# An attention and long-convolution backbone: value products issued two steps at a time, the exponentials' two half sums added on TensorE, reciprocals on a reshaped tile, the maxima's remainders in pairs, weight scalings on ScalarE

## The chip, the cores and the metric

One core of a Trainium2 chip runs the whole program. The metric is the device time of one execution in microseconds (us), lower is better; the time before is a median of three runs. Engines are named as in the profile: PE (TensorE, with PEld for its weight loads), DVE (VectorE), ACT (ScalarE), POOL (GpSimd), SP (SyncE, which issues the transfers).

## The reference, cut to what matters

Two layers over 1024 latent tokens of width 1024, with 256 context tokens before them as further keys. The first layer is attention, the second a gated long convolution; the change touches the attention alone. Its two kinds of heads have the same core:

```python
def one_block(qi):
    s = jnp.einsum("bqhgd,bkhd->bhgqk", _f32(qi), kf) * scale
    p = jax.nn.softmax(s, axis=-1)
    return jnp.einsum("bhgqk,bkhe->bqhge", p, vf)
...
o_a = block_attention(q_a..., k_a, v_a, GQA_HEAD_DIM ** -0.5)           # 8 heads, 2 key/value heads, width 64
o_m = block_attention(q_m..., k_m, v_m, (MLA_NOPE_DIM + MLA_ROPE_DIM) ** -0.5)   # 8 heads, width 96, values 64
o = jnp.concatenate([o_a..., o_m...], axis=-1)
return (o * jax.nn.silu(gate)) @ w_out
```

There are 1280 keys for each query. All is float32, and the norm weights are drawn large (factors of 8 on `attn_q_norm`, `attn_k_norm` and `mla_q_norm`), so scores are large and a row's maximum has to be subtracted before the exponential.

## The kernel before, in words

Queries stand in columns: a block of scores is [128 keys, 512 queries]. `groups` lists 32 groups, (kind, head, half of the queries): groups 0 to 15 are kind 0 (grouped-query heads), groups 16 to 31 kind 1 (latent heads). A group has five **steps**, each with two key tiles of 128.

One step of `attention()` (L1230 to L1288) does for each of its two key tiles j the score products into one of two [128, 1024] PSUM tiles `pw` (L1253; two passes of fp32r matmuls for kind 0, three for kind 1, so that products of split high and low parts add up to float32), then one exponential on ACT over both tiles (L1261, `PT`), a running sum of the exponentials (`add`, L1169: POOL adds the [128, 1024] tiles of steps 1 to 3, and of step 4 DVE adds one half and POOL the other), and the value products of the step before (`pv`, L1158, in full float32: four matmuls of 64 columns by 256 queries, two side by side in the array). `later` holds the steps whose value products are still to come.

Three further things run inside the steps:

- The **maxima of the next group**, `max_piece` (L980): 12 matmuls per group, for each of four query tiles three widths of keys, 512, 512 and 256, each into a PSUM bank from `pq()` and reduced on DVE (L989). Three of them go with each of steps 0 to 3. `max_all` (L991) reduces the [128, 12] to [128, 4], `max_rows` (L1003) turns that on PE (L1009, a float32 transpose) and DVE writes the negated rows into the next group's queries (L1014), where an extra row of the key operand adds them to the scores.
- The **end of the group before**: `add_last` (L1181) adds the two halves of the sum on DVE into `acs`; `gated` (L1206) multiplies the value products by the gate out of PSUM; `sums` (L1198) adds over keys with four matmuls by ones, one per query tile, side by side in strips of 32 (L1202), and DVE takes the reciprocal of [128, 128] of which four rows are used (L1204); `spread` (L1215) sends those rows to memory and back to 64 partitions; `scale_out` (L1224) multiplies on POOL, two groups later.
- A second generator, `mla_prep` (L1331), makes the latent heads' queries (`nope`, `pe`), keys (`key_stack`, L1308) and values (`Vm`, L1460 to L1479). Each begins with a scaling of weights by a norm vector and a split into a high and a low part. A third, `out_weights`, prepares the output projection's weights.

`Streams` (L70) runs these generators against a clock of estimated costs when the program is written, so the order on each engine is fixed in advance; an engine takes its instructions in that order and waits where one is not ready. A PSUM bank from `pq()` (three in rotation during attention: the fourth holds the value products of two groups, `pv2`) can be written again once its reader is done. Tiles with `bufs=1` (`acc`, `acs`, `R`, `rb`) are written again once the last reader is done.

## Time and profile before

| | |
|---|---|
| median of three runs | 1850.01 us (1847.22 to 1852.31) |
| the profiled execution's own time | 1850.4 us |
| its span in the profile | 1848.5 us |
| attention, groups 0 to 31 | from 490 to 1037 us of the span |
| PE, DVE, ACT, POOL busy over the span | 94%, 61%, 41%, 47% |
| chain of work that ended last | PE 54%, DVE 10%, DMA 5%, POOL 2%, ACT 2% |

"Busy" counts the records' durations. A matmul record lasts longer than the step from one matmul to the next (0.39 us against 0.23 us for 512 columns), because matmuls are pipelined. So the start times of neighbouring PE rows are what tells a matmul's cost, and an idle PE in a table has been waiting a little longer than the table says.

### The profile page before, as it was taken

Reading aid. Unit: us, or ns where it says so; the run is one execution under the profiler, and the core shown is the slowest. Engines: PE = TensorE matmul, PEld = TensorE weight load, DVE = VectorE, ACT = ScalarE, POOL = GpSimd, SP = SyncE. Lnnn points to the kernel's source line nnn. Section 1 sums busy time; section 2 is a strip of 40 time slices with the busy share of each in tenths; the row PEclk is TensorE's granted clock in tenths of the full one; section 3 lists DMA queues with packets and bytes.
Section 4 is the critical chain, followed back from the end, with each engine's and each line's share of the span. In section 5 each row is a group of like instructions: output and inputs, shape, how many; then the busy total and the mean of one; then the engine's idle time right before and its main releaser. Section 6 shows DMA issues by size and latency. Waiting matters only on the chain.

```text
span 1848.5 us, 25379 instructions
## 1 busy us (share of the span) xinstructions
PE 1744.1 (94%) x9360; PEld 1332.5 (72%) x9360; DVE 1136.7 (61%) x1646; ACT 749.9 (41%) x1250; POOL 866.2 (47%) x606
## 2 busy tenths in 40 slices
PE   7899999999999998899999999999999999889898
PEld 2677788977765665565656688888878888778676
DVE  5467657446777877777777423555676666555743
ACT  4878711253544544343443333243333343333332
POOL 2457622443378778566666453234243334334300
PEclk9999999999999999899999999999999999999999
DMA  7776688122120011001000215567778787787623
GB/s 248 231 225 217 201 260 271 56 80 80 36 58 24 13 44 29 27 21 34 19 22 29 77 69 149 166 172 219 219 205 235 227 244 204 204 239 217 202 93 112
DMA packets 243427, 253.18 MB, mean 137 GB/s; under 512 B 28191, under 2 KB 193087, under 8 KB 242887
## 3 DMA queue, kind: packets, MB, share of 16 engines
q1 hardware_dynamic: 241128, 249.47, 45.2%
q10 hardware_dynamic: 2176, 2.10, 0.4%
q8 instruction: 74, 1.21, 0.3%
q14 instruction: 49, 0.40, 0.1%
HBM read 169.65 MB, written 61.94 MB: 125 GB/s over the span
## 4 chain that ended last, share of the span: by engine, by line
PE 54%; DVE 10%; DMA 5%; POOL 2%; ACT 2%; issue 2%; SPq 1%; POOLq 0%; DVEq 0%; ACTq 0%
PE pw L1253 8%; PE pw L103 8%; PE pw L101 8%; PE pw L102 8%; PE pv L1166 6%; PE pq L988 3%; PE pq L101 2%; PE pq L102 2%; PE pq L103 2%; PE pq L1818 2%; DMA K<-Kd 2%; PE pq L1835 2%; DVE mx L989 2%; DMA bd<-cbT 1%; DMA ad<-caT 1%
## 5 line engine op out<-in xcount | busy, mean ns | idle before, releaser
L1261 ACT ACTIVATE PT<-pw 128x1024 f32<-128x1024 f32 x160 | 163.6, 1023 | 218.2 <-PE pw L1253 210.1
L989 DVE TENSOR_REDUCE mx<-pq 128x1 f32<-128x512 f32 (+1 forms) x384 | 215.5, 594 | 42.3 <-PE pq L988 38.7
L101 PE MATMUL pw<-h1h,wh 128*128 128x512 f32 x512 | 209.6, 409 | 0.0
L103 PE MATMUL pw<-h1h,wl 128*128 128x512 f32 x512 | 202.5, 396 | 3.6 <-POOL wl L1676 3.6
L102 PE MATMUL pw<-h1l,wh 128*128 128x512 f32 x512 | 200.8, 392 | 0.0
L1811 POOL TENSOR_TENSOR K<-K,skp 128x512 f32<-128x512 f32 x64 | 85.4, 1336 | 217.7 <-DMA K<-Kd 210.9
L1175 POOL TENSOR_TENSOR acc<-acc,PT 128x1024 f32<-128x1024 f32 x62 | 147.7, 2383 | 35.9 <-ACT PT L1261 33.7
L103 PEld LDWEIGHTS pw<-h1h,wl 128*128 128x128 f32 x512 | 96.5, 188 | 25.7 <-POOL wl L1676 4.3
L1821 DVE SCALAR_TENSOR_TENSOR cB<-pq,K 64x512 f32<-64x512 f32 x64 | 44.3, 693 | 110.6 <-PE pq L1818 36.6
L547 POOL TENSOR_TENSOR kacc<-kacc,kabs 128x512 f32<-128x512 f32 x56 | 72.2, 1289 | 83.8 <-ACT kabs L545 81.9
L102 PEld LDWEIGHTS pw<-h1l,wh 128*128 128x128 f32 x512 | 97.3, 190 | 17.9
L101 PEld LDWEIGHTS pw<-h1h,wh 128*128 128x128 f32 x512 | 97.3, 190 | 17.5
L1173 POOL TENSOR_TENSOR acc<-PT,PT 128x1024 f32<-128x1024 f32 x31 | 73.7, 2377 | 74.3 <-DVE acs L1184 63.7
L1676 POOL TENSOR_TENSOR wl<-wr,wh 128x1024 fp32r<-128x1024 f32 x32 | 78.6, 2455 | 54.5 <-ACT wh L1675 36.2
L1791 ACT COPY caT<-pq 128x512 f32<-128x512 f32 x64 | 37.6, 587 | 142.0 <-PE pq L103 101.9
L1166 PE MATMUL pv<-PT,Va 128*64 128x256 f32 x640 | 86.7, 392 | 2.3 <-DVE gT L1212 2.3
L1166 PE MATMUL pv<-PT,Vm 128*64 128x256 f32 x640 | 85.9, 391 | 0.0
L1852 DVE TENSOR_TENSOR cil<-spare,cih 128x512 fp32r<-128x512 f32 x64 | 57.1, 930 | 42.2 <-ACT cih L1851 42.2
L573 PE MATMUL pq<-au,FBk 128*128 128x256 f32 x256 | 68.3, 391 | 11.8 <-DVE kc L584 11.6
L1818 PE MATMUL pq<-cau,FB 128*128 128x128 f32 x512 | 69.7, 280 | 8.9 <-DVE cA L1824 7.9
L1835 PEld LDWEIGHTS pq<-cA,GB 128*128 128x128 f32 x512 | 67.6, 193 | 12.3 <-issue 7.1
L1837 ACT COPY cbT<-pq 128x512 f32<-128x512 f32 x64 | 37.3, 587 | 95.9 <-PE pq L1835 53.0
(444 smaller groups left out, 4727.1 us busy)
## 6 DMA issues: line engine op xcount, KB each, us to landing
K<-Kd SPq DMA_DIRECT2D x128, 256.0 KB
au<-aT SPq DMA_DIRECT2D x128, 128.0 KB
space<-in_ada_w_dram SPq DMA_DIRECT2D x32, 512.0 KB
wr<-in_hy_w_in_dram SPq DMA_DIRECT2D x32, 512.0 KB
ad<-caT SPq DMA_DIRECT2D x64, 256.0 KB
cau<-ad SPq DMA_DIRECT2D x32, 512.0 KB
bd<-cbT SPq DMA_DIRECT2D x32, 512.0 KB
spare<-bd SPq DMA_DIRECT2D x64, 256.0 KB
```

The costliest lines, as they stand in the source:

```text
L101: nc.tensor.matmul(ps, lh, rh, start=start, stop=False)
L102: nc.tensor.matmul(ps, lh, rl, start=False, stop=False)
L103: nc.tensor.matmul(ps, ll, rh, start=False, stop=stop)
L989: nc.vector.reduce_max(mxs[gi][:, p:p + 1], ps[:, :w], axis=AX.X)
L1166: nc.tensor.matmul(ps[64 * e:64 * e + 64, 0:256], vals[:, 2 * s + j], PT[:, j, 256 * e:256 * e + 256], start=s == 0 and j == 0, stop=s == ...
L1175: eng.tensor_tensor(accs[gi], accs[gi], PT, ALU.add)
L1253: nc.tensor.matmul(ps[:, 512 * j:512 * j + 512], l[:, kt * P:(kt + 1) * P], r, start=i == 0, stop=i == len(passes) - 1)
L1261: nc.scalar.activation(PT, ps.rearrange("p (a q) -> p a q", q=512), AF.Exp, scale=SC_A if kind == 0 else SC_M)
L1676: nc.gpsimd.tensor_tensor(wl, f(r), f(wh), ALU.subtract)
L1811: nc.gpsimd.tensor_tensor(K[:, 0], K[:, 0], B["skp"].unsqueeze(1).to_broadcast([P, 4, P]), ALU.add)
L1818: nc.tensor.matmul(ps[:, i * P:(i + 1) * P], FB[:, 4 * uc + i, :], au[:, 4 * (uc % 2) + i, :], start=True, stop=True)
L1835: nc.tensor.matmul(ps[:, i * P:(i + 1) * P], GB[:, 4 * uc + i, :], A1[:, i, :], start=True, stop=True)
```

## The change

- **Value products** are issued in bursts: where `(group + step)` is odd, those of the two oldest waiting steps; otherwise none (group 16: in steps 1 and 4).
- **Sums**: `add_last` and `acs` are gone. `sums` takes both halves of `acc` (now two buffers) as eight matmuls that accumulate, and stands in step 3 of an even group and step 2 of an odd one.
- **Reciprocals**: ACT copies the [128, 128] out of PSUM, a transfer brings the four used rows to [32, 16], DVE takes the reciprocal of that two steps or more later (`inverse`, in step 0), and `spread` follows from there. `scale_out` moves from step 0 to step 3. Groups 30 and 31 keep the old way.
- **Maxima**: the 256-wide remainders of two query tiles share one bank and one reduction (12 reductions become 10); pieces go as two or three per step, with one behind the burst; `max_all` moves from step 4 to the end of step 3, and the transpose in `max_rows` stands between the two key tiles' scores of step 4. In step 0 the first pass of both key tiles, which doesn't read the new rows, is issued ahead of the second.
- **Scalings**: the scalings by norm vectors go from DVE to ACT, the low parts of `ukl` and `uvl` from DVE to POOL, the high part in `nope` and half of the copies of `Vm` from DVE to ACT.

```diff
-    def max_piece(gi, p):
+    def max_piece(gi, i, j):
...
+        if j < 2:
+            nc.tensor.matmul(ps, tile_(i), K[:, 512 * j:512 * j + 512], start=True, stop=True)
+            nc.vector.reduce_max(m[:, i, j:j + 1], ps, axis=AX.X)
+        else:
+            for e in range(2):
+                nc.tensor.matmul(ps[:, 256 * e:256 * e + 256], tile_(i + e), K[:, 1024:1280], start=True, stop=True)
+            nc.vector.tensor_reduce(m[:, i:i + 2, 2], ps.rearrange("p (e k) -> p e k", e=2), AX.X, ALU.max)
...
-                accs[gi] = ap_.tile([P, 2, 512], F32, tag="acc", bufs=1, name=nm("acc"))
+                accs[gi] = ap_.tile([P, 2, 512], F32, tag="acc", bufs=2, name=nm("acc"))
...
-        def add_last(gi):
-            a = accs[gi]
-            accs[gi] = ap_.tile([P, 512], F32, tag="acs", bufs=1, name=nm("acs"))
-            nc.vector.tensor_tensor(accs[gi], a[:, 0], a[:, 1], ALU.add)
...
-            for i in range(4):
-                nc.tensor.matmul(pr[32 * i:32 * i + 32, 0:P], ones[:, 0:32], a[:, i * P:(i + 1) * P], start=True, stop=True)
-            Rs[gi] = ap_.tile([P, P], F32, tag="R", bufs=1, name=nm("R"))
-            nc.vector.reciprocal(Rs[gi], pr[:, 0:P])
+            for e in range(2):
+                for i in range(4):
+                    nc.tensor.matmul(pr[32 * i:32 * i + 32, 0:P], ones[:, 0:32], a[:, e, i * P:(i + 1) * P], start=e == 0, stop=e == 1)
+            R = ap_.tile([P, P], F32, tag="R", bufs=1, name=nm("R"))
...
+                nc.scalar.copy(R, pr[:, 0:P])
+                Rs[gi] = ap_.tile([32, 16], F32, tag="rc", bufs=2, name=nm("rc"))
+                nc.sync.dma_start(Rs[gi], R[0:P:32, :].rearrange("a (b q) -> a b q", q=16))
+
+        def inverse(gi):
+
+            rc = Rs.pop(gi)
+            nc.vector.reciprocal(rc, rc)
+            spread(gi, rc)
...
-                olds = [later.pop(0) for _ in range(len(later) - keep)]
+                burst = s in (1, 4) if gi == 16 else (gi + s) % 2
+                olds = [later.pop(0) for _ in range(len(later) - 1)] if burst else []
...
+                if s == 0:
+                    for j in range(2):
+                        scores(j, todo[:1])
+                    todo = todo[1:]
+                scores(0, todo)
...
                 if s == 0 and gi > 1:
+                    inverse(gi - 2)
+                if s == 3 and gi > 1:
                     scale_out(gi - 2)
...
-                if s == 1 and gi > 0:
-                    add_last(gi - 1)
+                if s == 1 + gi % 2 and gi > 0:
                     gated(gi - 1)
-                if s == 2 and gi > 0:
+                if s == 3 - gi % 2 and gi > 0:
                     sums(gi - 1)
...
+    def scaled_parts(wh, wl, r, k):
+
+        nc.scalar.activation(r, r, AF.Identity, scale=k)
+        nc.scalar.copy(wh, r)
+        nc.gpsimd.tensor_tensor(wl, r, f(wh), ALU.subtract)
...
-                    nc.vector.tensor_copy(A[0:64, c], raw)
+                    nc.scalar.copy(A[0:64, c], ps[b_])
...
-        nc.vector.tensor_scalar(r, r, kw, 0.0, ALU.mult, ALU.add)
+        nc.scalar.activation(r, r, AF.Identity, scale=kw)
...
-        nc.vector.tensor_tensor(uvl, r, f(uvh), ALU.subtract)
+        nc.gpsimd.tensor_tensor(uvl, r, f(uvh), ALU.subtract)
...
-            evac(Vm[:, kt, :], ps)
+            nc.scalar.copy(Vm[:, kt, :], ps)
```

Over the whole program the matmuls by ones go from 128 to 256 and no other product is added or removed. DVE loses 151 of its 1648 instructions, ACT gains 76 and POOL 9, and SP issues 30 more transfers.

**PE, group 7, from the sums of group 6 to the first scores of group 8, before.** `pw` are scores, L988 the maxima's pieces, L1202 the sums, L1166 value products (x4 is one step), L1009 the transpose of the maxima.

```order
L1202 MATMUL pq_5705<-acs_5679,ones 32x128 x4
L1253 MATMUL pw_5717<-Qa_4199,K_4188 128x512
L1253 MATMUL pw_5717<-Q_4194,K_4190 128x512
...
L988 MATMUL pq_5731<-K_4189,Qa_4200 128x256
L1166 MATMUL pv_4631<-PT_5667,Va 64x256 x4
L1253 MATMUL pw_5738<-Qa_4199,K_4188 128x512
...
L1009 MATMUL pq_5747<-ident,m_1097_5741 4x128
L1166 MATMUL pv_4631<-PT_5691,Va 64x256 x4
L1253 MATMUL pw_5755<-Qa_4200,K_4189 128x512
```

**The same place in the change.** L1277 are scores, L989 and L993 the pieces, L1212 the sums, L1180 value products, L1023 the transpose.

```order
L989 MATMUL pq_5694<-K_4189,Qa_4200 128x512
L1212 MATMUL pq_5699<-acc_5568,ones 32x128 x8
L1277 MATMUL pw_5713<-Qa_4199,K_4188 128x512
...
L989 MATMUL pq_5723<-K_4189,Qa_4200 128x512
L1277 MATMUL pw_5730<-Qa_4199,K_4188 128x512
L1277 MATMUL pw_5730<-Q_4194,K_4190 128x512
L1023 MATMUL pq_5733<-ident,m_1076_5727 4x128
L1277 MATMUL pw_5730<-Qa_4199,K_4188 128x512
L1277 MATMUL pw_5730<-Q_4194,K_4190 128x512
L1180 MATMUL pv_4627<-PT_5665,Va 64x256 x4
L1180 MATMUL pv_4627<-PT_5678,Va 64x256 x4
L1277 MATMUL pw_5749<-Qa_4200,K_4189 128x512 x2
```

The transpose stood directly ahead of value products, two matmuls of scores and one step of value products behind the last piece; now it stands between scores, two matmuls behind the last piece. In odd groups a piece also stands between the value products and the sums; in even groups the sums follow the value products directly. Counted over the attention, the unbroken runs of float32 matmuls among the fp32r ones go from 158 (125 of value products with or without sums, 31 with a transpose ahead, 2 of sums alone) to 127 (79 of value products, 17 of sums alone, 31 of a transpose alone).

**POOL, groups 14 and 15, before** (`acc` the running sums of exponentials `PT`; `gT<-gT,rb` is `scale_out`):

```order
L1173 TENSOR_TENSOR acc_6699<-PT_6641,PT_6670 128x1024
L1175 TENSOR_TENSOR acc_6699<-acc_6699,PT_6694 128x1024
L1175 TENSOR_TENSOR acc_6699<-acc_6699,PT_6728 128x1024
L1179 TENSOR_TENSOR acc_6699<-acc_6699,PT_6748 128x512
L1228 TENSOR_TENSOR gT<-gT,rb_6717 64x512
L1173 TENSOR_TENSOR acc_6819<-PT_6767,PT_6790 128x1024
```

**The same in the change:**

```order
L1187 TENSOR_TENSOR acc_6699<-PT_6641,PT_6661 128x1024
L1189 TENSOR_TENSOR acc_6699<-acc_6699,PT_6694 128x1024
L1250 TENSOR_TENSOR gT<-gT,rb_6651 64x512
L1189 TENSOR_TENSOR acc_6699<-acc_6699,PT_6710 128x1024
L1193 TENSOR_TENSOR acc_6699<-acc_6699,PT_6752 128x512
L1187 TENSOR_TENSOR acc_6815<-PT_6764,PT_6796 128x1024
```

`scale_out` now stands ahead of the group's last full addition, whose result DVE's half addition (L1192 in the change) reads in step 0 of the next group.

## Rows read from the trace of the kernel before

**Rows 1.** The page's first part: busy time of each engine, share of the span, instructions.

```profile
PE 1744.1 (94%) x9360; PEld 1332.5 (72%) x9360; DVE 1136.7 (61%) x1646; ACT 749.9 (41%) x1250; POOL 866.2 (47%) x606
```

**Rows 2.** Busy time by stretch: the stretch around group 16, and the sum over 490 to 1037 us, which is the attention (length, busy us of each engine, and in the first row the granted clock, DMA share and GB/s).

```profile
738.00:780.00 42.00, 33.33 (x158) 22.52 (x159) 29.56 (x41) 16.80 (x23) 19.61 (x11) 0.88 0.09 33
...
sum 547.00, PE 518.15 PEld 327.29 DVE 415.68 ACT 231.67 POOL 387.05; mean PE 172.72 PEld 109.10 DVE 138.56 ACT 77.22 POOL 129.02
```

**Rows 3.** PE in order of time in group 7, where no other work is mixed in: start us, us, engine, line, what, count. Two records stand for each float32 matmul, so x8 is four of them.

```profile
601.96 0.51 PE L988 MATMUL pq<-K,Qa 128*128 128x512 f32 x2
602.40 1.08 PE L1166 MATMUL pv<-PT,Va 128*64 128x256 f32 x8
603.41 0.43 PE L1202 MATMUL pq<-acs,ones 128*32 128x128 f32 x8
603.77 0.50 PE L1253 MATMUL pw<-Qa,K 128*128 128x512 f32 x1
604.11 0.39 PE L1253 MATMUL pw<-Q,K 128*128 128x512 f32 x1
604.34 0.39 PE L988 MATMUL pq<-K,Qa 128*128 128x512 f32 x1
...
607.51 0.27 PE L1009 MATMUL pq<-ident,m 128*4 128x128 f32 x1
607.72 1.08 PE L1166 MATMUL pv<-PT,Va 128*64 128x256 f32 x8
...
609.29 0.39 PE L988 MATMUL pq<-K,Qa 128*128 128x512 f32 x1
```

**Rows 4.** PE in order of time in group 16, where the value products of three steps follow each other.

```profile
766.80 2.81 PE L1166 MATMUL pv<-PT,Vm 128*64 128x256 f32 x24
769.54 0.45 PE L101 MATMUL pq<-ckh,ukh 128*64 128x512 f32 x1
```

**Rows 5.** What PE waited for between 490 and 1037 us: who <- what, us in total, times, longest.

```profile
PE pq L1202 <- DVE mx L989: 11.7, 8, 3.2
PE pq L988 <- DVE mx L989: 5.1, 9, 1.0
PE pq L102 <- DVE uvl L1472: 3.1, 1, 3.1
...
PE pq L988 <- ACT nraw L1381: 1.5, 1, 1.5
```

**Rows 6.** PE in order of time in group 16, as Rows 3; in brackets the idle time before and what ended it.

```profile
749.30 0.43 PE L1202 MATMUL pq<-acs,ones 128*32 128x128 f32 x8 [3.16 <-DVE mx L989]
...
756.12 0.80 PE L102 MATMUL pq<-uvl,ckh 128*128 128x512 f32 x1 [3.08 <-DVE uvl L1472]
...
757.14 0.63 PE L101 MATMUL pq<-uvh,ckh 128*128 128x512 f32 x1
757.57 0.63 PE L102 MATMUL pq<-uvl,ckh 128*128 128x512 f32 x1
```

**Rows 7.** DVE in order of time: in groups 7 and 8, and around the first products of `Vm` in group 16.

```profile
606.51 0.17 DVE L994 TENSOR_REDUCE m<-mx 128x4 f32<-128x12 f32 x1
607.82 0.68 DVE L1014 TENSOR_TENSOR Q<-pq,dneg 4x512 fp32r<-4x512 f32 x1 [1.14 <-PE pq L1009]
609.73 0.69 DVE L989 TENSOR_REDUCE mx<-pq 128x1 f32<-128x512 f32 x1 [1.22 <-PE pq L988]
...
746.65 1.88 DVE L1466 TENSOR_SCALAR uvr<-uvr,kw 128x512 f32<-128x512 f32 x1
...
753.38 2.69 DVE L1472 TENSOR_TENSOR uvl<-uvr,uvh 128x512 fp32r<-128x512 f32 x1
```

**Rows 8.** Groups of instructions by form between 490 and 1042 us: line, engine, operation, out<-in, shapes, count | busy us, mean ns of one | idle us before them and what ended most of it.

```profile
L989 DVE TENSOR_REDUCE mx<-pq 128x1 f32<-128x512 f32 x248 | 166.0, 685 | 38.1 <-PE pq L988 34.6
L1261 ACT ACTIVATE PT<-pw 128x1024 f32<-128x1024 f32 x160 | 163.6, 1023 | 218.2 <-PE pw L1253 210.1 <-POOL acc L1179 4.4 <-POOL acc L1175 1.7
L1175 POOL TENSOR_TENSOR acc<-acc,PT 128x1024 f32<-128x1024 f32 x62 | 147.7, 2383 | 35.9 <-ACT PT L1261 33.7
L1173 POOL TENSOR_TENSOR acc<-PT,PT 128x1024 f32<-128x1024 f32 x31 | 73.7, 2377 | 74.3 <-DVE acs L1184 63.7 <-ACT PT L1261 9.2 <-PE pw L1253 1.5
L989 DVE TENSOR_REDUCE mx<-pq 128x1 f32<-128x256 f32 x124 | 51.1, 412 | 0.0
L1228 POOL TENSOR_TENSOR gT<-gT,rb 64x512 f32<-64x512 f32 x31 | 41.4, 1337 | 10.6 <-DVE acc L1175 9.2 <-DMA rb<-rd 0.3
L1178 DVE TENSOR_TENSOR acc<-acc,PT 128x512 f32<-128x512 f32 x32 | 41.3, 1290 | 2.3 <-POOL acc L1175 1.9 <-ACT PT L1261 0.4
L1204 DVE RECIPROCAL R<-pq 128x128 f32<-128x128 f32 x32 | 30.5, 953 | 6.5 <-PE pq L1202 6.0
L1184 DVE TENSOR_TENSOR acs<-acc 128x512 f32<-128x512 f32 x32 | 25.2, 786 | 1.2 <-POOL acc L1179 1.2
L1315 DVE TENSOR_SCALAR ukr<-ukr,kw 128x64 f32<-128x64 f32 x8 | 11.1, 1390 | 0.1
L1381 ACT COPY nraw<-pq 64x512 f32<-64x512 f32 x16 | 9.3, 582 | 16.6 <-PE pq L103 14.1 <-POOL QB L1383 2.3
```

**Rows 9.** SP's transfers of a group's reciprocals: the issue of the one to memory, and of the one back, which waits until the first has landed.

```profile
751.07 0.55 SPq L1218 DMA_DIRECT2D rd<-R  x1
...
752.73 0.48 SPq L1222 DMA_DIRECT2D rb<-rd  x1
```

More of the change, by code (lines that the diff above doesn't have):

```diff
@@ L978, in backbone, with pieces_of @@
     mxs = {}
-    def max_piece(gi, p):
+    def max_piece(gi, i, j):
         kind, h, q = groups[gi]
         K, Q, _ = keys_of(kind, h)
-        i, j = p // 3, p % 3
-        if p == 0:
+        if gi not in mxs:
             mxs[gi] = kvp.tile([P, 12], F32, tag="mx", bufs=2, name=nm("mx"))
-        c0, w = ((0, 512), (512, 512), (1024, 256))[j]
+        m = mxs[gi].rearrange("p (i j) -> p i j", j=3)
         ps = pq()
-        nc.tensor.matmul(ps[:, :w], Q[:, (4 * q + i) * P:(4 * q + i + 1) * P], K[:, c0:c0 + w], start=True, stop=True)
-        nc.vector.reduce_max(mxs[gi][:, p:p + 1], ps[:, :w], axis=AX.X)
-        return w / 2400
+        tile_ = lambda i: Q[:, (4 * q + i) * P:(4 * q + i + 1) * P]
+        if j < 2:
[5 more added lines that the diff above has]
+            nc.vector.tensor_reduce(m[:, i:i + 2, 2], ps.rearrange("p (e k) -> p e k", e=2), AX.X, ALU.max)
+        return 0.213
+    def pieces_of(gi):
+        wide = deque((i, j) for i in range(4) for j in range(2))
+        rest = deque((i, 2) for i in (0, 2))
+        out = []
+        for s in range(4):
+            out.append([wide.popleft(), rest.popleft(), wide.popleft()] if (gi + s) % 2 else [wide.popleft(), wide.popleft()])
+        return out + [[]]
     def max_all(gi):
@@ L1055, in stacks @@
             if pr == 0:
-                for p in range(12):
-                    cost = max_piece(0, p)
+                for piece in sum(pieces_of(0), []):
+                    cost = max_piece(0, *piece)
                     yield cost, 0.6
@@ L1244, in attention, with scores @@
                 ps = pw()
-                nxt = list(range(3 * s, 3 * s + 3)) if gi + 1 < 32 and s < 4 else []
-                keep = HOLD if gi == 16 and s in (2, 3) else 1
-                olds = [later.pop(0) for _ in range(len(later) - keep)]
-                if any(x[:2] == (16, 0) for x in olds):
+                nxt = deque(pieces_of(gi)[s]) if gi + 1 < 32 else deque()
+                burst = s in (1, 4) if gi == 16 else (gi + s) % 2
+                olds = [later.pop(0) for _ in range(len(later) - 1)] if burst else []
+                if any(x[0] == 16 for x in olds):
                     yield lambda: "Vm" in done
-                for j in range(2):
+                def scores(j, some):
                     kt = 2 * s + j
-                    for i, (l, r) in enumerate(passes):
+                    for i, (l, r) in some:
                         nc.tensor.matmul(ps[:, 512 * j:512 * j + 512], l[:, kt * P:(kt + 1) * P], r,
                                          start=i == 0, stop=i == len(passes) - 1)
-                        cost += 0.213
-                    if j == 0 and nxt:
-                        cost += max_piece(gi + 1, nxt[0])
-                    elif j == 0 and gi + 1 < 32:
-                        max_all(gi + 1)
-                PT = ap_.tile([P, 2, 512], F32, tag="PT", bufs=5, name=nm("PT"))
-                nc.scalar.activation(PT, ps.rearrange("p (a q) -> p a q", q=512), AF.Exp, scale=SC_A if kind == 0 else SC_M)
+                todo = list(enumerate(passes))
+                cost += 0.426 * len(passes)
+                if s == 0:
[3 more added lines that the diff above has]
+                scores(0, todo)
                 if nxt:
-                    cost += max_piece(gi + 1, nxt[1])
+                    cost += max_piece(gi + 1, *nxt.popleft())
                 if s == 4 and gi + 1 < 32:
@@ L1266, in attention @@
                     cost += 0.1
+                scores(1, todo)
+                PT = ap_.tile([P, 2, 512], F32, tag="PT", bufs=5, name=nm("PT"))
+                nc.scalar.activation(PT, ps.rearrange("p (a q) -> p a q", q=512), AF.Exp, scale=SC_A if kind == 0 else SC_M)
+                if nxt and (len(nxt) > 1 or not olds):
+                    cost += max_piece(gi + 1, *nxt.popleft())
+                if nxt and s == 3:
+                    cost += max_piece(gi + 1, *nxt.popleft())
                 if later:
@@ L1270, in attention @@
                 prev = PT
-                if nxt:
-                    cost += max_piece(gi + 1, nxt[2])
                 for old in olds:
@@ L1276, in attention @@
                         cost += 0.46
+                while nxt:
+                    cost += max_piece(gi + 1, *nxt.popleft())
+                if s == 3 and gi + 1 < 32:
+                    max_all(gi + 1)
                 if s == 0 and gi > 1:
+                    inverse(gi - 2)
+                if s == 3 and gi > 1:
                     scale_out(gi - 2)
@@ L1348, in uq_split @@
             for k in range(2):
-                nc.vector.tensor_scalar(r[:, k], r[:, k], cqw[:, k:k + 1], 0.0, ALU.mult, ALU.add)
+                nc.scalar.activation(r[:, k], r[:, k], AF.Identity, scale=cqw[:, k:k + 1])
             nc.scalar.copy(wh, r)
```

18 lines of the change are left out of this document (8 added, 10 removed).

## The prediction

> **What bounds the kernel now.** I read the page's first part, then busy time by stretch, PE in order of time, PE's waits, and the groups by form. PE is busy for 94% of the span [rows 1], and the change touches only the attention: 547 us, of which the table leaves PE 547.0 - 518.2 = 28.9 us idle [rows 2]. So two things are to be had there: those idle microseconds, and matmul time that isn't products. All else after 1037 us stays as it is, and what PE gains in the attention moves the end one for one.
>
> The idle time has one main cause. PE stands at the sums and at pieces of maxima and waits for DVE: 11.7 + 5.1 us, and 3.1 us for `uvl` [rows 5]. DVE works for 416 of the 547 us [rows 2], on short instructions in fixed order, and each late one holds up the reductions behind it. Two of its instructions take far longer than their size explains: the `ukr` scaling of 64 columns has a mean of 1.39 us, the half addition 1.29 us [rows 8]; `uvl` took 2.69 us [rows 7].
>
> Matmul time that isn't product is in the turns between fp32r scores and float32 products. In group 7 nothing waits, so the steps between starts are prices [rows 3]. A score takes 0.23 us (604.11 to 604.34). The two pieces at 601.96, 512 and 256 columns, should take 0.35 us and take 0.44: 0.09 for entering float32. One step of value products takes 1.01 us (602.40 to 603.41); three in a row take 2.74 [rows 4], so one more costs 0.865, and a lone one 0.15 more than that. The first score afterwards takes 0.34 (603.77 to 604.11): 0.11 for leaving. A turn costs 0.35 us.
>
> **The change part by part.**
>
> *Bursts, transpose and sums on PE.* The runs of float32 go from 158 to 127, not to half, because the transposes and half of the sums now stand alone. Before: 125 runs with value products x 0.35, 31 that begin with the transpose x 0.26 (the transpose takes its own 0.21 us, 607.51 to 607.72, in either place, and I see no entry price on it), 2 lone sums x 0.20: 52.2 us. After: 79 x 0.35, 17 x 0.20, 31 lone transposes x 0.11: 34.5. That saves 17.7 us. The sums grow by 32 sets of four: the first set takes 0.36 (603.41 to 603.77), less the entry 0.27; at least 0.22, a quarter of 0.865 for half the columns and twice the strips; at most 0.36. I take 0.27, the nearest row less its entry: 8.6 us (7 to 11.5). Net **-9 us** (-6 to -11).
>
> *DVE's load.* Gone per group: `acs` 0.79; the reciprocal of [128, 128], 0.95, for one of [32, 16], for which no row stands (0.12 by an eighth of the columns, up to 0.95); four reductions of 256 (0.41) for two of 512 (0.685): 0.27. Some 1.9 of 13 us per group, and over the attention the scalings too. Reductions arrive from PE at best every 0.69 us in kind 0 (piece and two scores) and DVE takes 0.67 for each (166.0/248): it keeps up, without much to spare.
>
> The waits at the sums should go: they no longer need `acs`, and stand a step or more later. `uvr`'s 1.88 us on DVE, which kept PE until 749.30 [rows 6, 7], moves to ACT. I count all idle time as open, 28.9 us and 3 more (a record of 0.39 us covers the first 0.16 of each of some 19 waits [rows 5]): **-32 us**, and enter below what stays or is new. After the two long waits PE ran at the lower level: 0.43 us per matmul (757.14 to 757.57) for 0.23, and 0.88 as mean clock over 42 us [rows 2], 10 us at 1.2 GHz, of which 3 were waiting: **-3.5 us**.
>
> *New: the transpose in odd groups.* There the last piece is followed by two scores alone. DVE begins 0.44 us after the piece (609.29 to 609.73 [rows 3, 7]), reduces for 0.67, and `m` takes 0.17 [rows 7]: 1.28 us. PE gets there after piece and scores, 0.69 us in kind 0 and 0.92 in kind 1: 8 x 0.6 + 7 x 0.35 = **+7 us**. Even groups have a burst in between and pay nothing. The transposed rows (0.68 on DVE, 607.82) are needed after four scores in even groups, behind the burst in odd ones: the reordered first passes cover them; without these PE would stand 0.4 us.
>
> *`uvl` on POOL.* After the exponential of step 2 POOL has an addition (2.38), `scale_out` (1.34) and `uvl`, between 1.2 (half of an addition) and 2.7 (what DVE took): from the end of those scores 1.2 + 2.4 + 1.3 + 1.3 = 6.2 us. PE has step 3 and the sums, 3.2 us. **+3 us** (0 to 5), in place of 3.1, and at even chance the lower clock again: **+1.5**.
>
> *The rest.* Group 16 keeps PE's wait for `nope`'s copies, 1.5 us [rows 5]: ACT now makes two of 0.58 for each one on DVE before. ACT's copy of the sums (nearest row 0.58 for 64x512) goes between exponentials, and ACT is busy for 232 of 547 us; the program loads no more tables for it. ACT copies a tile of `Vm` in some 0.6 us (the same nearest row), PE makes one in 0.69. POOL loses the 63.7 us pause that one `acc` buffer forced on it [rows 8]. For waits that DVE and POOL still cause where `mla_prep` runs I leave 6 us of the 32. **+7.5 us.**
>
> **Sum:** -9 - 32 - 3.5 + 7 + 3 + 1.5 + 7.5 = -25.5. The profiled execution took 1850.4 us, 0.4 above the median of the runs: **1825 us**.
>
> **Two pages weighed.** The half addition's 1.29 us [rows 8] is nearly twice the 0.79 of `acs`, which has the same shape. The Trainium skill, "SBUF — State Buffer", section "Who interferes with whom", has a rule on it: a DVE instruction with two SBUF inputs and a GpSimd instruction that reads SBUF exclude each other, and the second waits for the whole of the first. By that rule the change also harms, since POOL pauses less; the second rival carries it.
>
> The transfer to memory is issued 1.66 us before the one back, which waits for it [rows 9]. The Trainium skill, "DMA: Bandwidth & Descriptors", section "Anatomy of one DMA", gives about 2.0 us of fixed cost per transfer: by it three hops would be an estimated 6 us, by the row 5; the sum is the same by both as long as `scale_out` isn't late.
>
> **The rivals.**
>
> *Slower: POOL holds DVE (10%).* `scale_out` now stands ahead of the last full addition, which DVE's half addition needs in step 0 of the next group; DVE is in order, so all maxima wait behind it. In an odd group the reciprocal comes some 3.5 to 4.5 us after the start and `rb` 1.66 x 2 plus two issues of 0.5 later, at 8 to 9; POOL gets to `scale_out` at about 10.4 (step 0 with its burst 3.4, the scores of step 1 1.1, an exponential 1.02 [rows 8], two additions of 2.4). It decides from the point at which `rb` is over 1.5 us late. PE then loses what DVE can't hide behind a burst, some 1.5 us in each of 30 groups: 45 us, 1870. Against it: that slack, and `scale_out` waited only 0.3 us for its transfer before [rows 8]. For it: SP issues transfers of 0.55 us in one queue, where `pe_out`'s stand ahead of some.
>
> *DVE stays the limit (15%).* If each of 31 half additions waited out an addition of 2.38, DVE would lose 31 x (2.38 + 0.68 - 1.29) = 55 us, as much as it saves, and half of the idle time would stay: 13 us more, **1838**. For it: four reductions in a row leave 0.02 us of slack each. Against it: DVE's mean load.
>
> *No gain in all (8%).* The waits go elsewhere, in full: -9 - 3.5 + 7 + 4 = **1849**.
>
> *More (10%).* The new waits of 7 and 3 us and the clock don't show: **1813**.
>
> **How the numbers follow.** Forecast 57% (1816 to 1834 by the bounds above: 5 us for products, 5 for `uvl` and the clock, 6 for the rest). The range takes in the better case mostly, and the second rival, and leaves out 10% above and some 8% below and between: **1808 to 1846**. A measurement of this kernel can tell 0.3%, 5.6 us, from no change. Faster by more: 57 + 10 + most of 15 = 80%. Within: 8 and a little of the second rival, 10%. Slower: 10%.
>
> **What would show it.** Right: idle PE in the attention near 14 us; pairs of value products 1.88 us long; waits at the sums gone; transposes in odd groups waiting 0.3 to 0.6 us for `m`, in even ones not; one wait of about 3 us at `uvl`; POOL's first addition no longer waiting for DVE. Wrong: POOL waiting for `rb`, half additions waiting for POOL, PE waiting for maxima in every group, or runs of float32 whose turns cost other than 0.35 us.

## Result and profile after

The changed kernel took 1821.26 us (median of 4 runs, 1819.12 to 1832.92), the kernel before 1848.62 (4 runs, 1844.94 to 1852.31): a ratio of 0.9865, with a 95% interval of 0.9818 to 0.9911. The profiled run took 1821.09 us, with a span of 1819.3.

Busy time by stretch of the kernel after: the first 16 groups, group 16 with parts of its neighbours, the rest of the attention (length, busy us of PE, PEld, DVE, ACT and POOL, granted clock, DMA share, GB/s).

```profile
486.00:735.00 249.00, 237.86 (x1517) 159.02 (x1518) 155.48 (x268) 130.46 (x184) 196.92 (x117) 1.00 0.11 31
735.00:780.00 45.00, 39.82 (x223) 27.71 (x220) 17.46 (x31) 22.99 (x34) 26.51 (x16) 0.92 0.10 35
780.00:1006.00 226.00, 223.24 (x1442) 152.68 (x1440) 138.15 (x236) 101.12 (x139) 162.29 (x87) 1.00 0.09 27
```

The same stretches before had these rows:

```profile
490.00:742.00 252.00, 244.31 (x1396) 152.37 (x1394) 201.14 (x347) 112.84 (x136) 199.26 (x116) 1.00 0.11 32
742.00:780.00 38.00, 29.93 (x142) 20.42 (x142) 25.92 (x37) 15.09 (x21) 16.27 (x9) 0.87 0.09 33
780.00:1037.00 257.00, 243.91 (x1394) 154.50 (x1392) 188.62 (x302) 103.75 (x126) 171.52 (x86) 1.00 0.07 23
```

PE's idle time is the length of a stretch less PE's busy time. In the last stretch it goes from 13.1 to 2.8 us, around group 16 from 8.1 to 5.2. In the first 16 groups it grows, from 7.7 to 11.1. DVE's load falls from 416 to 311 us.

What PE waited for in the attention of the kernel after (between 486 and 1010 us: who <- what, us in total, times, longest), to be held against [rows 5]:

```profile
PE pq L1023 <- DVE m L1008: 6.7, 13, 0.8
PE pq L101 <- POOL uvl L1508: 4.1, 1, 4.1
PE pq L100 <- ACT QA L1418: 2.5, 3, 0.9
PE pq L989 <- DVE mx L990: 1.2, 1, 1.2
PE pq L989 <- ACT QA L1418: 0.9, 1, 0.9
PE pq L1212 <- DVE acc L1193: 0.8, 1, 0.8
```

The 11.7 us of waiting for DVE at the sums are gone, but for 0.8 behind the last group. In their place stand the waits for `m` (4.0 us of them in the first 16 groups), for `uvl`, and for ACT's copies of `nope`.

The measure for what follows is the time between the starts of the first and the last of the attention's 160 exponentials, a row of ACT: before and after.

```profile
L1261 ACT ACTIVATE PT<-pw x160: 1013/1023/1030, 490.2 to 1032.5; 128x1024 f32<-128x1024 f32 x160
```

```profile
L1294 ACT ACTIVATE PT<-pw x160: 1004/1026/1032, 486.4 to 1001.5; 128x1024 f32<-128x1024 f32 x160
```

542.3 us became 515.1: -27.2. I count its 3.8 us earlier start as scatter: the two traces differ from the first loads of `ada_w` on, e8 and e12 below, which run the same instructions up to group 16, start 2.0 us apart, and in 14 profiles the span outside this measure lies between 1302 and 1318 us. A median of whole runs carries that scatter. The attention hardly does, though each figure is of one profiled run: a pair of groups in the second half repeats within 0.02 us, and the first 16 groups took 240.8 us in e8 and 240.7 in e12. Within the attention, from first exponential to first exponential, groups 0 to 15 went from 248.3 to 245.9, group 16 from 36.3 to 30.8, groups 17 to 31 from 257.6 to 238.3. Over two thirds of the gain lie in the second half, where of the other work only the keys of the latent heads and the output projection's weights are mixed in.

PE in order of time in group 7 of the kernel after (start us, us, engine, line, what, count), against [rows 3]:

```profile
594.85 0.40 PE L993 MATMUL pq<-K,Qa 128*128 128x256 f32 x2
595.17 1.95 PE L1180 MATMUL pv<-PT,Va 128*64 128x256 f32 x16
597.05 0.49 PE L989 MATMUL pq<-K,Qa 128*128 128x512 f32 x1
597.48 0.65 PE L1212 MATMUL pq<-acc,ones 128*32 128x128 f32 x16
598.05 0.50 PE L1277 MATMUL pw<-Qa,K 128*128 128x512 f32 x1
598.39 0.39 PE L1277 MATMUL pw<-Q,K 128*128 128x512 f32 x1
...
599.77 0.39 PE L1277 MATMUL pw<-Q,K 128*128 128x512 f32 x1
600.83 0.27 PE L1023 MATMUL pq<-ident,m 128*4 128x128 f32 x1 [0.67 <-DVE m L1008]
600.86 0.48 PE L1277 MATMUL pw<-Qa,K 128*128 128x512 f32 x1
601.17 0.40 PE L1277 MATMUL pw<-Q,K 128*128 128x512 f32 x1
```

Two steps of value products take 1.88 us (595.17 to 597.05), as forecast. Eight matmuls by ones take 0.57 (597.48 to 598.05), 0.22 more than the four before, where 0.27 was entered; from a piece of 512 into them it takes 0.43, so 0.20 for the entry. The lone transpose delays the score behind it by 0.03 and the next one by 0.08, with 0.67 of waiting ahead of it.

### The profile page after: what moved, and what is told of

Same layout as the page of the kernel before. It is cut to its first block, busy times and chain, and to the rows that moved or that the text cites. A ratio compares the mean times of both kernels' runs of the same rounds, so it can differ in the third digit from the quotient of the medians.

```text
span 1819.3 us, 25906 instructions
## 1 busy us (share of the span) xinstructions
PE 1725.1 (95%) x9616; PEld 1346.1 (74%) x9616; DVE 1029.7 (57%) x1495; ACT 774.3 (43%) x1326; POOL 865.6 (48%) x615
## 4 chain that ended last, share of the span: by engine, by line
PE 57%; DVE 7%; DMA 5%; POOL 3%; issue 2%; ACT 2%; SPq 1%; DVEq 0%; POOLq 0%; ACTq 0%
PE pw L1277 8%; PE pw L102 8%; PE pw L100 8%; PE pw L101 8%; PE pv L1180 7%; DMA K<-Kd 4%; PE pq L989 3%; PE pq L100 2%; PE pq L101 2%; PE pq L102 2%; PE pq L1871 2%; PE pq L1854 2%; DVE mx L990 2%; PE pq L1212 1%; POOL wl L1712 1%
## 5 line engine op out<-in xcount | busy, mean ns | idle before, releaser
L990 DVE TENSOR_REDUCE mx<-pq 128x1 f32<-128x512 f32 x256 | 170.9, 683 | 112.9 <-PE pq L989 111.1
L101 PEld LDWEIGHTS pw<-h1l,wh 128*128 128x128 f32 x512 | 97.0, 189 | 17.8
L1180 PE MATMUL pv<-PT,Va 128*64 128x256 f32 x640 | 77.9, 385 | 0.0
L1180 PE MATMUL pv<-PT,Vm 128*64 128x256 f32 x640 | 77.7, 385 | 0.0
```

Source lines behind the costliest of these rows:

```text
L101: nc.tensor.matmul(ps, lh, rl, start=False, stop=False)
L990: nc.vector.reduce_max(m[:, i, j:j + 1], ps, axis=AX.X)
L1180: nc.tensor.matmul(ps[64 * e:64 * e + 64, 0:256], vals[:, 2 * s + j], PT[:, j, 256 * e:256 * e + 256], start=s == 0 and j == 0, stop=s == ...
```

## Experiments

"Attention" is first to last exponential in the profiled run; ratios are to the kernel before.

| kernel | median us | ratio, 95% interval | attention us | groups 0-15 | 16 | 17-31 |
|---|---|---|---|---|---|---|
| before | 1848.6 | | 542.3 | 248.3 | 36.3 | 257.6 |
| changed | 1821.3 | 0.9865, 0.9818 to 0.9911 | 515.1 | 245.9 | 30.8 | 238.3 |
| e1 every step | 1838.2 | 0.9933, 0.9906 to 0.9961 | 525.5 | 250.8 | 28.1 | 246.7 |
| e2 before, scalings only | 1830.0 | 0.9909, 0.9885 to 0.9933 | 524.4 | 246.8 | 30.2 | 247.4 |
| e3 scalings on DVE | 1829.8 | 0.9911, 0.9887 to 0.9934 | 521.8 | 248.6 | 33.3 | 239.8 |
| e4 late transpose | 1815.7 | 0.9828, 0.9799 to 0.9857 | 508.5 | 243.1 | 30.9 | 234.6 |
| e5 halves on DVE | 1838.1 | 0.9930, 0.9908 to 0.9952 | 526.8 | 255.7 | 29.0 | 242.1 |
| e6 unpaired | 1823.3 | 0.9856, 0.9819 to 0.9893 | 517.3 | 248.2 | 30.8 | 238.3 |
| e7 old reciprocal | 1827.7 | 0.9879, 0.9834 to 0.9923 | 516.0 | 249.3 | 26.2 | 240.5 |
| e8 two bursts | 1805.1 | 0.9761, 0.9725 to 0.9796 | 500.3 | 240.8 | 27.4 | 232.1 |
| e9 two waits | 1820.1 | 0.9849, 0.9820 to 0.9878 | 510.3 | 248.5 | 23.5 | 238.3 |
| e10 e8 and e9 | 1810.6 | 0.9813, 0.9782 to 0.9843 | 503.1 | 243.6 | 27.4 | 232.1 |
| e11 scaling in step 4 | 1820.2 | 0.9847, 0.9824 to 0.9871 | 511.4 | 247.3 | 25.8 | 238.3 |
| e12 e8, early `uvh` | 1806.3 | 0.9756, 0.9727 to 0.9784 | 497.5 | 240.7 | 24.7 | 232.1 |

**e1: value products in every step again.**

```
-                burst = s in (1, 4) if gi == 16 else (gi + s) % 2
-                olds = [... range(len(later) - 1)] if burst else []
+                keep = 3 if gi == 16 and s in (2, 3) else 1
+                olds = [later.pop(0) for _ in range(len(later) - keep)]
```

> The changed kernel with its value products in every step again (runs of four matmuls instead of eight; three steps of group 16 stay together, as before the change). The order has 204 runs of float32 matmuls instead of 127. Theory (a turn costs 0.35 us, entry, lone step and exit together): 77 x 0.35 = 27 us slower than the changed kernel, some 1848, and the pairs of steps no longer 1.88 us long but 2 x 1.01. Rival (the gain came from DVE's waits alone, and a turn is covered by waits that PE has anyway): under 10 us slower, below 1832. Second rival (bursts give PE the cover for the wait of the transpose): more than 35 us slower.

The attention took 10.4 us more than in the changed kernel, and the median of whole runs 16.9: between the theory's 27 and the rival's "under 10". PE in order of time in e1:

```profile
882.82 0.40 PE L989 MATMUL pq<-K,QA 128*128 128x512 f32 x1
883.15 1.08 PE L1180 MATMUL pv<-PT,Vm 128*64 128x256 f32 x8
884.16 0.50 PE L1277 MATMUL pw<-QB,K 128*128 128x512 f32 x1
884.50 0.40 PE L1277 MATMUL pw<-QA,K 128*128 128x512 f32 x1
```

A single step costs 1.01 (883.15 to 884.16), its entry 0.10 and its exit 0.11, so the turn's price stands in the rows. The balance of a pair of groups in the second half gives it again: 17.73 + 16.23 = 33.96 us with ten runs of value products, against 15.90 + 17.03 = 32.93 with five, 0.54 of that waiting for `m` (0.38 in the table and the 0.16 that a matmul's record covers): (33.96 - 32.93 + 0.54)/5 = 0.31 us. What holds the total down is cover: with products in every step no transpose waits (the group of L1023 shows 0.0 us of idle time), nor does any piece wait for `nope`'s copies, and group 16 takes 2.8 us less. So 77 turns fewer are worth some 24 us, and 14 of them don't show. PE's idle time in the attention accounts for 9 of these: 10.3 us in e1, 19.1 in the changed kernel.

**e2: the kernel before with the scalings alone.**

```
-        nc.vector.tensor_scalar(r, r, box["kw"], 0.0, ALU.mult, ALU.add)
+        nc.scalar.activation(r, r, AF.Identity, scale=box["kw"])
...
-        nc.vector.tensor_tensor(wl, r, f(wh), ALU.subtract)
+        nc.gpsimd.tensor_tensor(wl, r, f(wh), ALU.subtract)
```

(and so for the queries' weights, `uvr`, `uvl`, the copies of `nope` and of `Vm`)

> The kernel before with one part of the change alone: the scalings and the splits behind them (ukr, ukl, the queries' weights, uvr, uvl, the copies of nope and of Vm) on ACT and POOL as in the changed kernel. Theory (waits at the sums in even groups of the second half come from DVE's scaling of ukr, which holds the reductions; 1.1 to 1.75 us in an interval that should be 0.31 or 0.23, some 2 us in each of 7 groups): 10 to 18 us faster than before, some 1835, and those waits gone. Rival (the waits come from the half addition and the addition of halves, which this kernel keeps): at most 5 us faster, and the waits at the sums remain.

The attention took 17.9 us less, at the theory's upper end; the waits at the sums are gone but 0.5 us. In their place PE waited 7.2 us for ACT's copies of `nope`. Of the 17.9 us, 10.2 are in groups 17 to 31, where of all that this kernel moves only six scalings of `ukr` and the six splits behind them run.

**e3: the changed kernel with the scalings back on DVE** (e2's edit reversed).

> The changed kernel with all scalings and splits back on DVE as before the change. Theory (with the sums a step later and the addition of halves gone, DVE has room for them; the waits for nope's copies on ACT, 3.4 us, and the 4.1 us at uvl go, uvr on DVE comes back with some 2 us): within 5 us of the changed kernel. Rival (the scalings held the reductions and their removal is most of the gain): 12 us or more slower, with PE waiting for maxima or for m in the even groups of the second half.

6.7 us more in the attention, a little over the theory's 5 and under the rival's 12. Without the scalings the other edits give 20.5 us, alone the scalings give 17.9, together 27.2: they overlap by 11. Of the overlap 8.7 lie in groups 17 to 31 (17.8 + 10.2 - 19.3), where of the scalings and splits only `ukr`'s run. POOL, then DVE, in order of time in the kernel before:

```profile
797.23 2.38 POOL L1173 TENSOR_TENSOR acc<-PT,PT 128x1024 f32<-128x1024 f32 x1 [3.15 <-DVE acs L1184]
```

```profile
796.41 0.67 DVE L1184 TENSOR_TENSOR acs<-acc 128x512 f32<-128x512 f32 x1
797.01 0.85 DVE L1212 TENSOR_TENSOR gT<-pv,gT 64x256 f32<-64x256 f32 x2
797.78 1.88 DVE L1315 TENSOR_SCALAR ukr<-ukr,kw 128x64 f32<-128x64 f32 x1
```

POOL's addition, freed by `acs`, starts at 797.23 and ends at 799.61. DVE's scaling of 64 columns starts 0.55 us into it and ends at 799.66. In six of its eight places it takes 1.65 to 1.89 us and ends so, within 0.06 us of POOL's addition. DVE in e3, where POOL's first addition waits for the exponentials alone:

```profile
856.21 0.85 DVE L1234 TENSOR_TENSOR gT<-pv,gT 64x256 f32<-64x256 f32 x2
856.98 0.24 DVE L1341 TENSOR_SCALAR ukr<-ukr,kw 128x64 f32<-128x64 f32 x1
857.54 0.22 DVE L1343 TENSOR_TENSOR ukl<-ukr,ukh 128x64 fp32r<-128x64 f32 x1 [0.31 <-ACT ukh L1342]
```

The same instruction takes 0.24 there (mean 0.26 of 8, against 1.39 [rows 8]): POOL's addition has ended 0.38 us before it. Moving the scaling to ACT and no longer making POOL wait for `acs` (with its second buffer for `acc`) are two ways to take away one wait, so they count once where both are made.

**e4: the transpose of odd groups behind the second tile's scores.**

```
-                if s == 4 and gi + 1 < 32:
+                if s == 4 and gi + 1 < 32 and gi % 2 == 0:
                     max_rows(gi + 1)
                 scores(1, todo)
+                if s == 4 and gi + 1 < 32 and gi % 2:
+                    max_rows(gi + 1)
```

> The changed kernel, but in odd groups the transpose of the maxima stands behind the second key tile's scores of step 4 and directly ahead of the value products, not between the two tiles. Theory (PE waits for m there, 0.54 us in each of 7 groups of the second half and about 0.8 in the first; the scores cover 0.46 to 0.69 of it; 15 of 127 float32 runs merge at 0.11 each): 5 to 9 us faster than the changed kernel, some 1814, and the interval from a score to the transpose back at 0.23. Rival (DVE is the limit, and what PE gains there it loses at the next reductions): within 2 us. Second rival (the transposed rows come too late for the next group's scores): slower.

6.6 us less, as the theory had it; the wait for `m` fell from 6.7 to 1.1. What PE gained in the first half (2.9) it kept. The next group's scores don't wait for the rows.

**e5: DVE adds the halves again.**

```
+        def add_last(gi):
+            a = accs[gi]
+            accs[gi] = a[:, 0]
+            nc.vector.tensor_tensor(a[:, 0], a[:, 0], a[:, 1], ALU.add)
...
-            for e in range(2): ... a[:, e, i * P:(i + 1) * P], start=e == 0, stop=e == 1)
+            for i in range(4): ... a[:, i * P:(i + 1) * P], start=True, stop=True)
```

> The changed kernel with one part undone: DVE adds the two halves of the sums again (in place, 31 instructions of some 0.8 us, in step 1 of the next group), and PE adds four strips instead of eight. Theory (DVE has room since the scalings left it, and the four further matmuls cost PE 0.2 to 0.27 us in each of 32 groups): 3 to 8 us faster than the changed kernel. Rival (without the addition on PE the waits at the sums and at the pieces come back): 4 us or more slower, with PE waiting for DVE at the sums. In the attention alone (first to last exponential) the changed kernel took 515.1 us.

The theory fell: 11.7 us more. The rival had the direction, not the place: PE waits 12.0 us for a bank of maxima at the paired pieces (13 times, longest 2.6), not at the sums. The addition is short only while POOL rests. DVE, then POOL, in e5:

```profile
879.43 0.68 DVE L1209 TENSOR_TENSOR acc<-acc 128x512 f32<-128x512 f32 x1
...
896.17 1.74 DVE L1209 TENSOR_TENSOR acc<-acc 128x512 f32<-128x512 f32 x1
```

```profile
879.70 2.65 POOL L1187 TENSOR_TENSOR acc<-PT,PT 128x1024 f32<-128x1024 f32 x1 [5.16 <-ACT PT L1298]
...
894.97 2.39 POOL L1187 TENSOR_TENSOR acc<-PT,PT 128x1024 f32<-128x1024 f32 x1
```

At 879.43 POOL is idle: 0.68. POOL's own addition, which starts 0.27 later, then takes 2.65 instead of 2.39. At 896.17 POOL adds until 897.36, and DVE ends 0.55 after that. The gating and three reductions stand behind it. The Trainium skill, "SBUF — State Buffer", section "Who interferes with whom", says that DVE with two SBUF inputs, or in a mode that uses both of its ports (which it says a `tensor_scalar` can enter), shares a port with GpSimd's reads, and that whichever comes second waits for the whole of the first. These rows and the scaling's agree; the gating of the value products, which reads PSUM and SBUF, took its 0.85 for two beside POOL's addition at 797.23.

**e6: remainders unpaired** (twelve reductions, three pieces in every step).

```
...
-        return out + [[]]
+        return [[(s, 0), (s, 1), (s, 2)] for s in range(4)] + [[]]
```

> The changed kernel with the remainders of 256 keys unpaired: twelve reductions in a group, three pieces in each step, as before the change. DVE has 0.27 us more in each of 31 groups. Theory (kind 1 has no wait for maxima but the transpose, kind 0 is close to DVE's limit): within 4 us of the changed kernel, what there is of it in the first 16 groups. Rival (the pairs and the uneven steps of two and three pieces are what keeps DVE ahead): 8 us or more slower, in both halves.

2.2 us more, all in the first 16 groups, as the theory had it.

**e7: the reciprocal of [128, 128] on DVE, `scale_out` in step 0.**

```
-                nc.scalar.copy(R, pr[:, 0:P])
...
+            nc.vector.reciprocal(R, pr[:, 0:P])
+            spread(gi, R[0:P:32, :])
```

> The changed kernel with the reciprocal of 128 columns on DVE again (0.95 us in place of 0.23), spread at once, and the multiplication by it on POOL in step 0 of the group after, as before the change. Theory (DVE has room in the second half, in the first it costs part of 0.7 us in each group; POOL's order of before did not hold DVE): 0 to 8 us slower. Rival (where the multiplication stands now, POOL holds the half addition, 12.2 us of DVE's waits, and the old place is the better one): faster than the changed kernel.

0.9 us more, as the theory had it, but the sum of two things: 5.5 us in the other groups (PE waits 12.6 us for `m`), and 4.6 less in group 16, where `scale_out` no longer stands ahead of `uvl`. The rival's mechanism is there too: DVE's waits for POOL fall from 12.2 to 5.4 us.

**e8: two bursts in every group, three steps in step 4 and two in step 1.**

```
-                burst = s in (1, 4) if gi == 16 else (gi + s) % 2
+                burst = s in (1, 4)
...
                         pv(*old[:3], j)
                         cost += 0.46
+                    if s == 4 and gi + 1 < 32 and old is olds[0]:
+                        max_rows(gi + 1)
...
-                if s == 3 - gi % 2 and gi > 0:
+                if s == (1 if gi == 31 else 4) and gi > 0:
                     sums(gi - 1)
```

> The changed kernel with two bursts in every group, three steps of value products in step 4 and two in step 1 (as group 16 has them already), the transpose inside the burst of step 4 and the sums at its end; four pieces of maxima in step 1, two in the others; the reciprocal one step later and the multiplication on POOL in step 4. The order has 62 runs of float32 matmuls instead of 127, and no lone transpose or sums. Theory (a turn of value products 0.30 to 0.35 us, a lone set of sums 0.20, a lone transpose 0.11, and 6.7 us of waiting for m): 15 to 20 us faster than the changed kernel, some 1803, with 497 us from the first to the last exponential. Rival (three steps without a burst leave DVE's reductions and POOL's additions behind, and PE waits there instead): within 5 us. Second rival (POOL, behind in the short steps, holds the buffers of the exponentials): slower than the changed kernel.

14.8 us less than the changed kernel, at the theory's lower edge and 3 us over its 497; 1805 us, faster than both kernels. PE in order of time in e8, and the engines' busy time by stretch:

```profile
846.28 1.08 PE L1180 MATMUL pv<-PT,Vm 128*64 128x256 f32 x8
847.30 0.27 PE L1023 MATMUL pq<-ident,m 128*4 128x128 f32 x1
847.50 1.95 PE L1180 MATMUL pv<-PT,Vm 128*64 128x256 f32 x16
849.38 0.64 PE L1212 MATMUL pq<-acc,ones 128*32 128x128 f32 x16
```

```profile
488.00:729.00 241.00, 233.83 (x1499) 156.75 (x1497) 151.52 (x265) 127.63 (x182) 193.07 (x115) 1.00 0.11 32
729.00:765.00 36.00, 32.46 (x182) 23.30 (x183) 16.72 (x31) 22.06 (x33) 21.48 (x14) 1.00 0.14 45
765.00:985.00 220.00, 220.00 (x1437) 152.15 (x1436) 137.81 (x234) 101.24 (x138) 166.72 (x89) 1.00 0.09 27
```

In the last stretch PE has no idle time left in the table; the wait for `m` is gone.

**e9: two of the new waits taken away.**

```
-        yield 0, U1
         nc.scalar.copy(uvh, r)
...
-        nc.gpsimd.tensor_tensor(uvl, r, f(uvh), ALU.subtract)
+        nc.vector.tensor_tensor(uvl, r, f(uvh), ALU.subtract)
...
-                    nc.scalar.copy(A[0:64, c], ps[b_])
+                for A, B, raw in raws:
+                    nc.scalar.copy(A[0:64, c], raw)
```

> The changed kernel with two of its new waits taken away: uvl on DVE again, its cast to uvh issued directly behind the scaling on ACT; and of nope's four copies on ACT the last two read SBUF, not the bank, so that the bank is free after two. Theory (PE waits 4.1 us for uvl and 3.4 us for the copies): 4 to 8 us less from the first to the last exponential than the changed kernel's 515.1, some 1815. Rival (what PE gains there it waits for DVE a little later): within 2 us.

4.8 us less, at the theory's lower edge, and the rival has its part: group 16 gains 7.4, the first 16 groups lose 2.6. DVE, then POOL, in group 14 of e9:

```profile
705.10 0.69 DVE L1192 TENSOR_TENSOR acc<-acc,PT 128x512 f32<-128x512 f32 x1 [4.80 <-POOL acc L1189]
```

```profile
696.43 2.37 POOL L1189 TENSOR_TENSOR acc<-acc,PT 128x1024 f32<-128x1024 f32 x1
698.88 1.29 POOL L1250 TENSOR_TENSOR gT<-gT,rb 64x512 f32<-64x512 f32 x1
700.24 2.51 POOL L1422 TENSOR_TENSOR QB<-nraw,QA 64x512 fp32r<-64x512 f32 x2
702.72 2.35 POOL L1189 TENSOR_TENSOR acc<-acc,PT 128x1024 f32<-128x1024 f32 x1
```

POOL, which has no pause between `nope`'s subtraction, the multiplication and the additions, sets the pace: DVE waits 4.80 us for POOL's last full addition (3.08 in the changed kernel), and PE 2.9 for a bank of maxima. This is the mechanism of the prediction's slower rival, in one place.

**e10: e8 and e9 together.**

> Two bursts in every group, and the two waits taken away as in the kernel beside it. Theory (the two gains add up): 3 to 6 us less than the 500.3 us that the two bursts took alone from the first to the last exponential, some 1800. Rival (group 16's wait for uvl is set by ACT's order of exponentials and casts, not by the engine that makes uvl): as the two bursts alone, 1805.

The gains don't add up: 2.8 us more than e8 alone. Group 16 took what it took in e8, and group 15 some 4 us more, for a reason that the rows show. DVE's half addition, then the last of four POOL instructions that run beside it without a pause:

```profile
709.25 4.92 DVE L1192 TENSOR_TENSOR acc<-acc,PT 128x512 f32<-128x512 f32 x1
```

```profile
711.27 2.35 POOL L1187 TENSOR_TENSOR acc<-PT,PT 128x1024 f32<-128x1024 f32 x1
```

DVE's addition starts while POOL multiplies and ends 0.55 us after the last of the four, so it takes 4.92 us instead of 0.68; the reductions stand behind it, and PE waits 2.6 us for a bank of maxima. In e8 the same addition takes 1.73. Which of the two edits brings this about was not tried apart. In group 16 PE waits less for `uvl` (1.7 us, 2.4 in e8), but then runs at the lower granted clock, 0.50, which it doesn't in e8:

```profile
742.00:744.00 2.00, 2.00 (x7) 1.51 (x6) 0.00 (x0) 0.79 (x2) 1.92 (x2) 0.50 0.25 72
```

**e11: `scale_out` in step 4, behind the last full addition.**

```
-                if s == 3 and gi > 1:
+                if s == 4 and gi > 1:
                     scale_out(gi - 2)
```

> The changed kernel with one thing moved: POOL's multiplication by the reciprocals stands in step 4, behind the last full addition, instead of step 3, ahead of it. Theory (in the first 16 groups POOL's queue holds DVE's half addition, 9.2 us of DVE's waits there, and reductions and PE behind it, and the multiplication's 1.29 us is a part of that): DVE's waits for POOL fall from 12.2 to 6 us or less, and the first 16 groups take 2 to 5 us less than 245.9. Rival (DVE would be late there by its own load, or POOL by nope's subtractions): within 1 us.

The theory fell for the first 16 groups: DVE's waits for POOL went from 12.2 to 7.7 us, but these groups took 1.3 us more; why was not looked into. The attention gained 3.7 us all the same, by group 16, which took 5.0 less: PE's wait for `uvl` fell to 1.4, and the granted clock stayed at 1.00.

**e12: e8 with `uvh` cast directly behind the scaling of `uvr`.**

```
         nc.scalar.activation(r, r, AF.Identity, scale=kw)
-        yield 0, U1
         nc.scalar.copy(uvh, r)
```

> The two bursts in every group, with the cast to uvh issued directly behind the scaling of uvr on ACT, uvl still on POOL, and nope's copies as in the changed kernel. Theory (group 16 waits 2.4 us for uvl since ACT makes uvh only behind the next exponential, 3.2 us after the scaling): group 16 takes 2 to 4 us less than 27.4, the rest as with the two bursts, some 1803. Rival (POOL's addition stands ahead of uvl then): group 16 as before, 1805.

Group 16 took 2.7 us less and the rest the same to 0.1; the wait for `uvl` is gone. POOL makes `uvl` at 732.35, ahead of an addition that stood ahead of it in e8. Its attention is the shortest of all, 2.8 us below e8's; by the times of whole runs, which overlap, the two can't be told apart.

Two parts of the change were not undone by themselves: the second buffer of `acc`, and the order of the first passes in step 0.

## Why the prediction was right

The time fell in the range, 3.7 us below the forecast, by the steps that it named. Two of their sizes were off: the turns saved 6 us more than forecast, the idle time 5 us less, and that these nearly cancel is luck. I hold the steps against the 27.2 us of the attention.

*Turns: -9 forecast, about -15.* The mis-sized term is the lone transpose. I charged its own 0.21 us "in either place", and 0.11 more where it stands alone. Ahead of value products it costs its 0.21 (607.51 to 607.72 [rows 3]); between scores it delays the next two starts by 0.03 and 0.08 only (600.83, 600.86, 601.17), 0.11 in all. For 31 transposes that is 31 x (0.21 + 0.11 - 0.11) = 6.5 us that I charged too much. The sums grew by 0.22 instead of 0.27 (1.6 in favour), the 16 lone ones enter at 0.20 instead of 0.09 (1.8 against): -9.1 - 6.5 - 1.6 + 1.8 = -15.4. The turn itself, 0.35, is confirmed by e1's rows, with 0.31 in its balance.

*Idle time: -14.5 net, -9.8 by the stretches.* 28.9 us became 19.1, not "near 14". In the second half the forecast holds: the waits at the sums went, what stays is `m`. In the first half waits were exchanged: 4.0 for `m`, 3.4 for `nope`'s copies on ACT, the rest for maxima and smaller things. I had left 7.5 us for such things in all, and `nope`'s copies alone held a bank in four places, not one; e2 has the same wait, 7.2 us. The reason that I gave, short instructions on DVE that take far too long, holds by e2: 10.2 us in groups 17 to 31, where only `ukr`'s scaling and split move.

*The transpose in odd groups: +7 forecast, 6.7 measured* in the table (0.67 in group 7), or some 8.8 with the 0.16 that a record covers at each of the 13 waits; e4 takes most of it away. This wait and the one at `uvl` are parts of the -9.8.

*`uvl`: +3 forecast, 4.1 measured*, and the clock. POOL did what I wrote (addition 2.35, `scale_out` 1.26, `uvl` 1.26); what I missed stands ahead of it on ACT:

```profile
738.50 0.73 ACT L1502 ACTIVATE uvr<-uvr,kw 128x512 f32<-128x512 f32 x1 [3.85 <-DMA uvr<-in_w_ukv_dram]
739.13 1.00 ACT L1294 ACTIVATE PT<-pw 128x1024 f32<-128x1024 f32 x1
```

ACT takes its instructions in order: it waits for the load of `uvr`, and the exponential of step 2, the last of whose scores starts at 737.37, stands behind the scaling. The whole is 7.5 us from the end of the scores where I had 6.2. PE's stretches after the wait:

```profile
742.00:744.00 2.00, 0.00 (x0) 0.00 (x0) 0.00 (x0) 0.00 (x0) 1.89 (x2) 0.83 0.01 1
744.00:750.00 6.00, 4.63 (x11) 3.67 (x12) 0.00 (x0) 1.76 (x3) 4.80 (x3) 0.50 0.22 87
```

The granted clock is 0.50, the level of 1.2 GHz, and from the first product at 745.37 on eleven steps between matmuls take 4.83 us, where at 0.23 each they took 2.5: 2.3 us. With the 3.5 us that I entered for the old place gone, this is -1.2 where -2 was entered. That the lower clock came again was a toss-up in the forecast and stays one: it followed the wait of 4.1 us here and one of 1.7 in e10, and not one of 2.4 in e8.

Together -15.4 - 9.8 - 1.2 = -26.4, of the -27.2 measured.

*The rivals.* "POOL holds DVE" is there in part. Its condition, a late `rb`, didn't come about: in groups 2 to 30 `scale_out` never waited for its transfer. DVE waits for POOL 12.2 us in all (7 times, longest 3.1), mostly in the first half (9.2), the longest there in group 14 behind `nope`'s subtractions, and PE loses a part only. "DVE stays the limit" supposed that each half addition would wait out an addition of POOL; its mean fell from 1.29 [rows 8] to 0.95 us, and 20 of the 32 took under 1.0. The Trainium skill's rule on the shared port held in the rows, but the prediction weighed it at the half addition alone, where the change would harm (1.29 us is 1.6 times the 0.79 of `acs`, not nearly twice; free, either takes 0.67). The scaling of `ukr` was a victim too, 1.39 us where e3 has 0.26, and there the change helps.

*The transfers.* The Trainium skill's 2.0 us per transfer, which the prediction set against the row's 1.66, stand in its section "Anatomy of one DMA" for transfers issued by GpSimd; those of the reciprocals are issued by SyncE, so the row is the nearer price. Nothing hung on it, as `scale_out` wasn't late.

## What to carry to other kernels

Where an instruction takes many times what its size explains, look at what the neighbour engine runs at that moment and what released it: a buffer freed by DVE can start the very POOL instruction that then holds DVE. Where POOL runs several instructions without a pause, one of DVE's can be held through all of them, as in e10. A burst saves its turns only as far as other work covers what it leaves bare, so move the waits (here the transpose) into the bursts, as e8 does. Compare the stretch that an edit touches, not whole runs, when the rest scatters by more than the effect.
